# A gated SSD layer: when each group's gate is normed and scaled, where its x tiles lie, and when the sample state is loaded

## The chip, the cores and the metric

The kernel runs on one NeuronCore of a Trainium2 chip. The metric is the device time of one execution in microseconds (us). Five engines work beside each other: TensorE (PE; its weight loads are listed apart as PEld), VectorE (DVE), ScalarE (ACT), GpSimd (POOL) and SyncE (SP). In this kernel every DMA is issued by SyncE, in the order of its instruction list. Each engine runs its own list in order and waits on semaphores for the others.

## The reference

One step of a streaming encoder with two layers, over a prompt of 1024 tokens and a sample chunk of 32 tokens that share all weights. Layer 0 mixes with a Mamba-2 SSD scan, layer 1 with stick-breaking attention; each is followed by a squared-ReLU MLP. The change lies in layer 0, whose mixer is, cut short:

```python
zxbcdt = u @ in_w                                   # z 2048, x 2048, B 1024, C 1024, dt 32 columns
xbc, new_conv = causal_conv(xbc, conv_state, conv_w, conv_b)      # 4 taps, then silu
# per chunk, heads in 8 groups of 4, h is the state of a head:
y_diag = einsum('btsg,btsgr,bsgrp->btgrp', cb, decay, xdt_c)
y_off  = einsum('btgn,bgrpn,btgr->btgrp', c_c, h, exp(a_cs))
h_new  = h * exp(a_cs[:, -1]) + einsum('bsgn,bsgr,bsgrp->bgrpn', b_c, decay_end, xdt_c)
y = (y + d_skip * x_h) * silu(z)                    # the gate
yg = y.reshape(bsz, seqlen, SSD_GROUPS, 256)
yg = yg * rsqrt(mean(yg * yg, axis=-1) + EPS)       # norm over a group's 256 columns
return (yg * norm_w) @ out_w, new_conv, h_new
```

The scan starts from zero for the prompt and from the given `ssm_state` for the sample. Both final states are outputs.

## The kernel before

**Tiling.** Everything is kept transposed: a tile is 128 features by 1056 tokens (1024 of the prompt, 32 of the sample). A float32 product is done in three passes over a high and a low half of both operands (L184), so one tile of the input projection, for 128 output features, is 8 x 3 x 3 = 72 matmuls of 128x352: three token groups of 24, each into its own PSUM tile `ps_i`. `gemm` returns such a tile as six thunks of 12 matmuls, two for each token group; the evacuation follows in the second. Ahead of the first, the weights are loaded (`ws_i`) and split into halves by ScalarE (L143) and GpSimd (L144).

**Groups.** The layer has eight groups of four heads. Group g needs six projection tiles: B, C, x0 and x1 (`conv_tile`) and z0 and z1 (`z_tile`). `conv_tile` multiplies by `rstd` into a padded row `pre` (L409, L412), runs the four taps (ScalarE L423, VectorE L425 twice, L427 and L428) and silu as a tanh (L429, L430). Its result `s_<g><kind>` goes to one of eight tiles h0 to h7, four for even groups and four for odd ones. The tap sums, the tanh of z and the gate's scratch `gs` share the tag "cv", which has two buffers.

**Scan.** `scan_thunks(g)` walks nine chunks, eight of 128 prompt tokens and chunk 8 with the sample's 32. `stage_a(c)` puts C times B and the transposes of x0, x1 and B into one PSUM tile `pa` (L469 to L472) and makes from it the decay matrix L, the scaled inputs `xd`, the copy `bt`, and `ab`, the decayed C (ScalarE L487, GpSimd L488). `stage_b(c)` multiplies them into `pb` (L504, L509, and L512 with the state h), adds the new state (L520), and adds the result to the x tiles in place (L523). For chunk 8 it first loads the sample's state `h0` (L497, L498) into a tile of the state's own rotation of three.

**Gate.** `gate(g)` returns three thunks: a multiplies the x tiles by z and sums their squares (GpSimd and ScalarE); b sums over the partitions on TensorE (`ss_g`), takes the reciprocal root on VectorE (L558 and the nine operations L214 to L223, each 128x264) and spreads it over all partitions through DRAM (L244 out, L247 back); c scales both x tiles (L564) and stores them to `yn_d` (L566), from where the output projection loads them after the last group.

**Order.** Iteration g of the loop at L610 makes a main list: the z tiles of group g-1, then B, C, x0 and x1 of group g+1, with the gate's thunks a, b, c of group g-1 ahead of B, C and x0. `weave` lays the 18 thunks of `scan_thunks(g)` between the 36 of the main list, starting after the third. In the last iteration z of group 7 and the first quarter of an output projection take the place of the convolutions. So the programme's order is written out here; the framework's scheduler then orders each engine's list from it, and the pools' tags decide who waits for whose buffer.

Of the kernel before, what the change touches and what calls it, by code (L numbers as in the profile page):

```python
# [7 lines left out]
F32 = mybir.dt.float32  # L8
# [10 lines left out]
T = SEQ + DEC  # L19
# [75 lines left out]
def hybrid_step(ctx: ExitStack, tc: tile.TileContext, xt, cst, cbf, w_in, w_dt, w_out, w_up0, w_dn0, w_qkv, w_o,  # L95
# [3 lines left out]
    dma = nc.sync.dma_start  # L99
# [4 lines left out]
    hx = ctx.enter_context(tc.tile_pool(name="hx", bufs=1))  # L104
# [193 lines left out]
    def ssd_layer():  # L298
# [4 lines left out]
        with st:  # L303
# [91 lines left out]
            slots = {}  # L395
            cnt = [0]

            def conv_tile(g, kind, xs=None):

                ct = {"x0": 2 * g, "x1": 2 * g + 1, "B": 16 + g, "C": 24 + g}[kind]  # L400
                slot = {"B": 0, "C": 1, "x0": 2, "x1": 3}[kind]
                fi = 6 * g + slot
                p = pre[cnt[0] % 2]
                cnt[0] += 1

                def evac(gi, ps):
                    lo, hi = gi * GW, (gi + 1) * GW
                    if hi <= SEQ:
                        ve.tensor_tensor(p[:, 3 + lo:3 + hi], ps, rstd[:, GRP[gi]], op=ALU.mult)  # L409
                    else:  # L410
                        n = SEQ - lo
                        ve.tensor_tensor(p[:, 3 + lo:3 + SEQ], ps[:, :n], rstd[:, lo:SEQ], op=ALU.mult)  # L412
                        ve.tensor_tensor(p[:, 6 + SEQ:], ps[:, n:], rstd[:, SEQ:], op=ALU.mult)
                        post()

                def post():
                    gp.tensor_copy(p[:, 3 + SEQ:6 + SEQ], cs[:, C_SC + 3 * ct:C_SC + 3 * ct + 3])
                    gp.tensor_copy(cvo[:, ct, 0:3], p[:, SEQ:SEQ + 3])
                    gp.tensor_copy(cvo[:, ct, 3:6], p[:, T + 3:T + 6])
                    n = SEQ + 3 + DEC  # L420
                    a = qp.tile([128, T + 6], F32, name=f"cv_{g}{kind}", tag="cv", bufs=2)
                    w = [cwh[:, 4 * ct + i:4 * ct + i + 1] for i in range(4)]
                    sc.activation(a[:, :n], p[:, 0:n], AF.Identity, scale=w[0], bias=cwh[:, 128 + ct:129 + ct])  # L423
                    for i in (1, 2):
                        ve.scalar_tensor_tensor(a[:, :n], p[:, i:i + n], w[i], a[:, :n], op0=ALU.mult, op1=ALU.add)  # L425
                    o = hx.tile([128, T], F32, name=f"s_{g}{kind}", tag=f"h{4 * (g % 2) + slot}")
                    ve.scalar_tensor_tensor(o[:, :SEQ], p[:, 3:3 + SEQ], w[3], a[:, :SEQ], op0=ALU.mult, op1=ALU.add)  # L427
                    ve.scalar_tensor_tensor(o[:, SEQ:], p[:, 6 + SEQ:], w[3], a[:, SEQ + 3:n], op0=ALU.mult, op1=ALU.add)  # L428
                    sc.activation(a[:, :T], o, AF.Tanh)  # L429
                    ve.scalar_tensor_tensor(o, a[:, :T], 1.0, o, op0=ALU.add, op1=ALU.mult)  # L430
                    slots[g, kind] = o

                return gemm(w_in[fi], xs or [xg[k] for k in range(KD)], pg, evac, f"i{fi}", gmajor=pa is not None or kind == "C")
# [23 lines left out]
            def scan_thunks(g):  # L457

                out = []
                box = {}  # L460

                def stage_a(c):
# [2 lines left out]
                    B, C, x0, x1 = (slots[g, k] for k in ("B", "C", "x0", "x1"))  # L465
                    ab = qp.tile([128, 4, 128], F32, name=f"ab_{g}_{c}", tag="ab", bufs=3)
                    dma(ab[:, :, :w], acs_d[4 * g:4 * g + 4, tk].partition_broadcast(128))
                    A = pa.tile([128, 512], F32, name=f"pa_{g}_{c}", tag="pa", bufs=2)
                    te.matmul(A[0:w, 0:w], B[:, tk], C[:, tk], start=True, stop=True)  # L469
                    te.transpose(A[0:w, 128:256], x0[:, tk], ident)  # L470
# [21 lines left out]
                def stage_b(c):  # L492
# [1 line left out]
                    tk = slice(128 * c, 128 * c + w)  # L494
                    L, xd, bt, ce = box.pop(c)
                    if c == 8:
                        h = qp.tile([128, 256], F32, name=f"h0_{g}", tag="hst", bufs=3)  # L497
                        dma(h, ssm0[g])  # L498
                    elif c == 0:
                        h = None  # L500
                    else:
                        h = box["h"]
# [35 lines left out]
            def gate(g):  # L538
# [1 line left out]
                ys = [slots[g, f"x{j}"] for j in range(2)]  # L540
                box = {}

                def scratch(n):
                    return qp.tile([128, T + 6], F32, name=f"{n}_{g}", tag="cv", bufs=2)[:, :T]

                def a():
                    box["s"] = [scratch(f"gs{j}") for j in range(2)]
                    e = ve if g == 7 else gp
                    for j in range(2):
                        e.tensor_tensor(ys[j], ys[j], slots[g, f"z{j}"], op=ALU.mult)  # L550
# [56 lines left out]
            def stage(b):  # L607
                return lambda i: (sp, f"pre{i}") if i < 2 else (qp, f"z{i - 2}")

            for g in range(8):  # L610
                main, side = [], scan_thunks(g)
                gt = gate(g - 1) if g > 0 else []
                if g > 0:
                    main += z_tile(g - 1, 0) + z_tile(g - 1, 1)
                if g < 7:
                    for k in ("B", "C", "x0", "x1"):
                        main += gt[0:1] + conv_tile(g + 1, k)
                        gt = gt[1:]
                else:
                    main += gt[0:1] + z_tile(7, 0) + gt[1:2] + z_tile(7, 1, False) + gt[2:3]  # L620
                    out0 = late(lambda: down_block(w_out[0], load_o(yn_d, 0, None, stage(0), 1), X, pg, "o0",
                                                   gmajor=True), 24)
# [1123 lines left out]
```

## Time and profile before

| what | number |
| --- | --- |
| median of three runs | 3028.87 us (3023.06 to 3031.92) |
| the profiled execution | 3030.64 us |
| its span, first to last instruction | 3028.8 us |
| mean granted clock of TensorE | 0.992 |
| instructions | 54974 |
| HBM read, written | 240.80 MB, 96.52 MB |
| stretch 0 to 90 us (first norm, tiles of group 0), PE busy | 82.56 us |
| stretch 155 to 728 us (six of the eight groups), PE busy | 551.50 of 573.00 us |
| the same stretch: VectorE, ScalarE, GpSimd busy | 443.20, 219.59, 362.73 us |
| stretch 728 to 870 us (end of the loop, output projection), PE busy | 140.13 of 142.00 us |

A busy share is the time in which an engine ran any instruction. The granted clock is the share of full speed that TensorE's throttle allowed; the trace gives it for windows of some 3.4 us. TensorE is the busiest engine of the loop, so what matters there is where it waits and at which clock it runs; a wait is read as the idle time ahead of an instruction with the instruction that ended it, printed as [us <-engine tile line].

### The profile page before, as it was taken

Reading aid. Unit: us, or ns where it says so; the run is one execution under the profiler, and the core shown is the slowest. Engines: PE = TensorE matmul, PEld = TensorE weight load, DVE = VectorE, ACT = ScalarE, POOL = GpSimd, SP = SyncE. Lnnn points to the kernel's source line nnn. Section 1 sums busy time; section 2 is a strip of 40 time slices with the busy share of each in tenths; the row PEclk is TensorE's granted clock in tenths of the full one; section 3 lists DMA queues with packets and bytes.
Section 4 is the critical chain, followed back from the end, with each engine's and each line's share of the span. In section 5 each row is a group of like instructions: output and inputs, shape, how many; then the busy total and the mean of one; then the engine's idle time right before and its main releaser. Section 6 shows DMA issues by size and latency. Waiting matters only on the chain.

```text
span 3028.8 us, 54974 instructions
## 1 busy us (share of the span) xinstructions
PE 2948.6 (97%) x22262; PEld 2800.2 (92%) x22262; DVE 2287.4 (76%) x3327; ACT 1291.2 (43%) x2207; POOL 645.9 (21%) x525
## 2 busy tenths in 40 slices
PE   9999999999999999999999999999999999999999
PEld 7899888998899999999998888888889999989999
DVE  7877787777847877788776577677777977788776
ACT  4433434333323433344333466666664433344331
POOL 2766666666200000000000023323230000000000
PEclk9999999999999999999999999999999999999999
DMA  4323333233532444365432322222234444465442
GB/s 135 75 69 79 70 84 83 75 73 105 179 115 99 154 157 142 124 199 165 142 111 101 90 82 75 66 77 67 65 113 159 145 148 153 135 200 160 134 132 76
DMA packets 185589, 349.28 MB, mean 115 GB/s; under 512 B 21132, under 2 KB 78328, under 8 KB 185336
## 3 DMA queue, kind: packets, MB, share of 16 engines
q1 hardware_dynamic: 185336, 345.77, 37.2%
q8 instruction: 175, 2.87, 0.4%
q14 instruction: 78, 0.64, 0.1%
HBM read 240.80 MB, written 96.52 MB: 111 GB/s over the span
## 4 chain that ended last, share of the span: by engine, by line
PE 76%; DVE 15%; issue 3%; DMA 3%; ACT 2%; POOL 0%; SPq 0%; DVEq 0%; ACTq 0%; POOLq 0%
PE ps_i L185 10%; PE ps_ua L878 9%; PE ps_ub L878 9%; PE ps_o L185 3%; PE ps_q L185 3%; PE ps_k L185 2%; PE o L1424 2%; PE wt L1408 2%; PE ps_o L166 2%; PE ps_lb L166 2%; PE ps_la L166 2%; DVE p L1371 1%; PE ps_p L185 1%; PE ps_v L185 1%; PE pb L509 1%
## 5 line engine op out<-in xcount | busy, mean ns | idle before, releaser
L185 PE MATMUL ps_i<-xh_n,wh_i 128*128 128x352 f32 x1056 | 359.2, 340 | 0.0
L185 PE MATMUL ps_i<-xh_n,wl_i 128*128 128x352 f32 x1056 | 343.4, 325 | 0.0
L185 PE MATMUL ps_i<-xl_n,wh_i 128*128 128x352 f32 x1056 | 343.2, 325 | 0.0
L1371 DVE TENSOR_TENSOR_SCAN p<-p 128x255 f32<-128x255 f32 (+7 forms) x128 | 193.4, 1511 | 90.2 <-ACT p L1369 89.2
L1373 POOL TENSOR_TENSOR b<-b,p 128x255 f32<-128x255 f32 (+7 forms) x128 | 165.4, 1293 | 378.0 <-DVE p L1371 232.6
L185 PEld LDWEIGHTS ps_i<-xh_n,wh_i 128*128 128x128 f32 x1056 | 201.6, 191 | 13.9 <-issue 11.7
L185 PEld LDWEIGHTS ps_i<-xl_n,wh_i 128*128 128x128 f32 x1056 | 203.0, 192 | 0.0
L185 PEld LDWEIGHTS ps_i<-xh_n,wl_i 128*128 128x128 f32 x1056 | 201.1, 190 | 0.0
L1245 POOL MEMSET qs<- 128x64 f32 x8 | 1.2, 152 | 868.7 <-PE ss_a L227 852.8
L477 ACT ACTIVATE L<-L,naT 128x128 f32<-128x128 f32 (+1 forms) x288 | 89.8, 382 | 164.7 <-POOL L L474 164.7
L1369 ACT ACTIVATE p<-z,qn_q 128x384 f32<-128x384 f32 (+4 forms) x192 | 104.7, 580 | 59.4 <-PE z L1400 29.0
L144 POOL TENSOR_TENSOR wl_i<-ws_i,wh_i 128x1024 fp32r<-128x1024 f32 x44 | 106.7, 2424 | 71.3 <-ACT wh_i L143 71.1
L474 POOL TENSOR_TENSOR L<-ab,cs 128x512 f32<-128x512 f32 (+1 forms) x72 | 102.7, 1427 | 55.9 <-PE pb L509 48.1
L1408 PE MATMUL wt<-cs,b 128*128 128x128 f32 x576 | 90.3, 280 | 15.4 <-DVE wts L1413 12.8
L1369 ACT ACTIVATE b<-z,qn_q 128x384 f32<-128x384 f32 (+4 forms) x192 | 104.5, 585 | 0.0
L729 ACT ACTIVATE d_a<-y_a 128x528 fp32r<-128x528 f32 x105 | 66.8, 640 | 87.2 <-DMA y_a<-q_da 15.9
L729 ACT ACTIVATE d_b<-y_b 128x528 fp32r<-128x528 f32 x105 | 66.3, 639 | 82.1 <-DMA y_b<-q_db 11.5
L1408 PEld LDWEIGHTS wt<-cs,b 128*128 128x128 f32 x576 | 64.9, 140 | 31.2 <-DVE wts L1413 14.0
L730 DVE TENSOR_TENSOR d_a<-y_a,d_a 128x528 fp32r<-128x528 f32 x105 | 73.2, 703 | 21.3 <-ACT d_a L729 21.2
L730 DVE TENSOR_TENSOR d_b<-y_b,d_b 128x528 fp32r<-128x528 f32 x105 | 73.2, 702 | 18.4 <-ACT d_b L729 18.3
L878 PE MATMUL ps_ub<-b_b,wh_b_raw 128*128 128x264 f32 x480 | 77.2, 282 | 0.0
L878 PE MATMUL ps_ua<-b_a,wh_a_raw 128*128 128x264 f32 x480 | 77.2, 282 | 0.0
(1667 smaller groups left out, 9441.7 us busy)
## 6 DMA issues: line engine op xcount, KB each, us to landing
y_a<-q_da SPq DMA_DIRECT2D x98, 264.0 KB
y_b<-q_db SPq DMA_DIRECT2D x98, 264.0 KB
ws_i<-in_w_in SPq DMA_DIRECT2D x48, 512.0 KB
ab<-acs_d SPq DMA_DIRECT2D x64, 256.0 KB
ws_a<-in_w_up SPq DMA_DIRECT2D x30, 512.0 KB
ws_b<-in_w_up SPq DMA_DIRECT2D x30, 512.0 KB
q_da<-t_a SPq DMA_DIRECT2D x26, 528.0 KB
q_db<-t_b SPq DMA_DIRECT2D x26, 528.0 KB
```

Of the source, the lines that this page charges most:

```text
L144: eng[0].tensor_tensor(lo, st, hi.bitcast(F32), op=ALU.subtract)
L166: te.matmul(box["ps"][g][:, :GW], a[:, c:c + 128], b[:, GRP[g]], start=(k == ks[0] and i == 0), stop=(k == ks[-1] and i == 2))
L185: te.matmul(box["ps"][:, :n], a[:, c:c + 128], b[:, grp[g]], start=(k == 0 and i == 0), stop=(k == nk - 1 and i == 2))
L474: gp.tensor_tensor(L[0:w, :, :w], ab[0:w, :, :w], cs[0:w, None, C_MASK:C_MASK + w].to_broadcast([w, 4, w]), op=ALU.add)
L477: sc.activation(L[0:w, h, :w], L[0:w, h, :w], AF.Exp, bias=naT[0:w, c, 4 * g + h:4 * g + h + 1])
L729: sc.activation(hi, x, AF.Copy)
L730: ve.tensor_tensor(lo, x, hi.bitcast(F32), op=ALU.subtract)
L878: te.matmul(ps[:, g, :QW], a[:, c:c + 128], b[:, QW * g:QW * g + QW], start=(first and n == 0 and i == 0), stop=(n == len(ks) - 1 and i == 2),
L1369: sc.activation(t[0:np_, c:c + w], ps[0:np_, :w], AF.Sigmoid, scale=sn[0:np_, f])
L1371: ve.tensor_tensor_scan(p[0:np_, 1:W][:, ::-1], p[0:np_, 1:W][:, ::-1], p[0:np_, 1:W][:, ::-1], 1.0, op0=ALU.mult, op1=ALU.bypass)
L1373: gp.tensor_tensor(b[0:np_, 0:W - 1], b[0:np_, 0:W - 1], p[0:np_, 1:W], op=ALU.mult)
L1408: te.transpose(ps[:, c, :], self.b[:, 128 * (c0 + c):128 * (c0 + c) + 128], ident)
```

## The change

It touches four things, all in `ssd_layer()`. What is computed stays the same.

1. The x tiles of a group rotate over three sets of two tiles (`XT`), where they had two sets: h2 and h3, h6 and h7, and a new pair in the pool `qp`. B and C keep their two sets.
2. The sample's state has a tile of its own, and its load is issued in `stage_a(4)` instead of in `stage_b(8)`.
3. The gate's scratch `gs0` and `gs1` have tiles of their own and no longer share "cv" with the convolutions.
4. Thunk a of a group's gate stays ahead of the next B tile. Thunks b and c wait for the next iteration, where they stand behind the first two thunks (24 matmuls) of the two z tiles.

```diff
--- before.py
+++ after.py
@@ -395,6 +395,8 @@
             slots = {}
             cnt = [0]
 
+            XT = [[(hx, "h2"), (hx, "h3")], [(hx, "h6"), (hx, "h7")], [(qp, "x20"), (qp, "x21")]]
+
             def conv_tile(g, kind, xs=None):
 
                 ct = {"x0": 2 * g, "x1": 2 * g + 1, "B": 16 + g, "C": 24 + g}[kind]
@@ -423,7 +425,8 @@
                     sc.activation(a[:, :n], p[:, 0:n], AF.Identity, scale=w[0], bias=cwh[:, 128 + ct:129 + ct])
                     for i in (1, 2):
                         ve.scalar_tensor_tensor(a[:, :n], p[:, i:i + n], w[i], a[:, :n], op0=ALU.mult, op1=ALU.add)
-                    o = hx.tile([128, T], F32, name=f"s_{g}{kind}", tag=f"h{4 * (g % 2) + slot}")
+                    pool, tag = (hx, f"h{4 * (g % 2) + slot}") if slot < 2 else XT[g % 3][slot - 2]
+                    o = pool.tile([128, T], F32, name=f"s_{g}{kind}", tag=tag, bufs=1)
                     ve.scalar_tensor_tensor(o[:, :SEQ], p[:, 3:3 + SEQ], w[3], a[:, :SEQ], op0=ALU.mult, op1=ALU.add)
                     ve.scalar_tensor_tensor(o[:, SEQ:], p[:, 6 + SEQ:], w[3], a[:, SEQ + 3:n], op0=ALU.mult, op1=ALU.add)
                     sc.activation(a[:, :T], o, AF.Tanh)
@@ -465,6 +468,9 @@
                     B, C, x0, x1 = (slots[g, k] for k in ("B", "C", "x0", "x1"))
                     ab = qp.tile([128, 4, 128], F32, name=f"ab_{g}_{c}", tag="ab", bufs=3)
                     dma(ab[:, :, :w], acs_d[4 * g:4 * g + 4, tk].partition_broadcast(128))
+                    if c == 4:
+                        box["h0"] = qp.tile([128, 256], F32, name=f"h0_{g}", tag="h0", bufs=1)
+                        dma(box["h0"], ssm0[g])
                     A = pa.tile([128, 512], F32, name=f"pa_{g}_{c}", tag="pa", bufs=2)
                     te.matmul(A[0:w, 0:w], B[:, tk], C[:, tk], start=True, stop=True)
                     te.transpose(A[0:w, 128:256], x0[:, tk], ident)
@@ -494,8 +500,7 @@
                     tk = slice(128 * c, 128 * c + w)
                     L, xd, bt, ce = box.pop(c)
                     if c == 8:
-                        h = qp.tile([128, 256], F32, name=f"h0_{g}", tag="hst", bufs=3)
-                        dma(h, ssm0[g])
+                        h = box["h0"]
                     elif c == 0:
                         h = None
                     else:
@@ -540,11 +545,8 @@
                 ys = [slots[g, f"x{j}"] for j in range(2)]
                 box = {}
 
-                def scratch(n):
-                    return qp.tile([128, T + 6], F32, name=f"{n}_{g}", tag="cv", bufs=2)[:, :T]
-
                 def a():
-                    box["s"] = [scratch(f"gs{j}") for j in range(2)]
+                    box["s"] = [qp.tile([128, T], F32, name=f"gs{j}_{g}", tag=f"gs{j}", bufs=1) for j in range(2)]
                     e = ve if g == 7 else gp
                     for j in range(2):
                         e.tensor_tensor(ys[j], ys[j], slots[g, f"z{j}"], op=ALU.mult)
@@ -607,16 +609,23 @@
             def stage(b):
                 return lambda i: (sp, f"pre{i}") if i < 2 else (qp, f"z{i - 2}")
 
+            gates = []
             for g in range(8):
                 main, side = [], scan_thunks(g)
-                gt = gate(g - 1) if g > 0 else []
                 if g > 0:
-                    main += z_tile(g - 1, 0) + z_tile(g - 1, 1)
+
+                    for j in range(2):
+                        z = z_tile(g - 1, j)
+                        main += z[:2] + gates[:1] + z[2:]
+                        gates = gates[1:]
+                    gates = gate(g - 1)
                 if g < 7:
                     for k in ("B", "C", "x0", "x1"):
-                        main += gt[0:1] + conv_tile(g + 1, k)
-                        gt = gt[1:]
+                        if k == "B" and gates:
+                            main.append(gates.pop(0))
+                        main += conv_tile(g + 1, k)
                 else:
+                    gt = gates
                     main += gt[0:1] + z_tile(7, 0) + gt[1:2] + z_tile(7, 1, False) + gt[2:3]
                     out0 = late(lambda: down_block(w_out[0], load_o(yn_d, 0, None, stage(0), 1), X, pg, "o0",
                                                    gmajor=True), 24)
```

From L409 on, the changed kernel's lines have moved by two to nine: L430 is now L433, L425 is L427, L448 is L451, L469 to L472 are L475 to L478, L478 is L484, L482 is L488, L520 is L525, L558 is L560, L564 is L566. L214 to L223 kept their numbers.

**The start of a group, TensorE.** These are TensorE's instructions around the first transposes of group 5, before: `ps_i` are the z tiles of group 4, `pa_0` is chunk 0, and L471 transposes x1, the last tile that the convolutions finished.

```order
L185 MATMUL ps_i_2_5242<-xh_n_233,wh_i_5185 128x352
L185 MATMUL ps_i_2_5242<-xl_n_234,wh_i_5185 128x352
L185 MATMUL ps_i_2_5242<-xh_n_233,wl_i_5186 128x352
L469 MATMUL pa_0_5257<-s_5C,s_5B 128x128
L470 MATMUL pa_0_5257<-cs,s_5x_5008 128x128
L471 MATMUL pa_0_5257<-cs,s_5x_5159 128x128
L472 MATMUL pa_0_5257<-cs,s_5B 128x128
L185 MATMUL ps_i_2_5242<-xh_n_262,wh_i_5185 128x352
```

The same place after the change; the second fence is the row sum of group 3's gate, which now stands a little ahead of it, between two token groups of the z tile.

```order
L185 MATMUL ps_i_1_5212<-xh_n_343,wh_i_5162 128x352
L185 MATMUL ps_i_1_5212<-xl_n_344,wh_i_5162 128x352
L185 MATMUL ps_i_1_5212<-xh_n_343,wl_i_5163 128x352
L475 MATMUL pa_0_5240<-s_5C,s_5B 128x128
L476 MATMUL pa_0_5240<-cs,s_5x_4987 128x128
L477 MATMUL pa_0_5240<-cs,s_5x_5138 128x128
L478 MATMUL pa_0_5240<-cs,s_5B 128x128
L185 MATMUL ps_i_2_5257<-xh_n_142,wh_i_5162 128x352
```

```order
L227 MATMUL ss_g_5193<-gs_3_4523,ones_71 32x264 x4
L185 MATMUL ps_i_1_5212<-xh_n_142,wh_i_5162 128x352
```

Between the last products of group 4 and these transposes stood two token groups of 24 matmuls and twelve of the third; now two token groups and the four matmuls of the row sum (eight records in the trace, where a float32 product takes two passes) stand there.

**The start of a group, VectorE.** Before, the end of x1's convolution stood among evacuations of z (L448):

```order
L425 SCALAR_TENSOR_TENSOR cv_5x_5155<-pre_90,cwh,cv_5x_5155 128x1059 x2
L448 SCALAR_TENSOR_TENSOR z_5214<-ps_i_0_5189,rstd 128x352
L427 SCALAR_TENSOR_TENSOR s_5x_5159<-pre_90,cwh,cv_5x_5155 128x1024
L428 SCALAR_TENSOR_TENSOR s_5x_5159<-pre_90,cwh,cv_5x_5155 128x32
L430 SCALAR_TENSOR_TENSOR s_5x_5159<-cv_5x_5155,s_5x_5159 128x1056
L448 SCALAR_TENSOR_TENSOR z_5214<-ps_i_1_5216,rstd 128x352
L478 TENSOR_TENSOR L_0_5262<-L_0_5262,pa_0_5257 128x512
```

After the change, at the same place:

```order
L427 SCALAR_TENSOR_TENSOR cv_5x_5134<-pre_90,cwh,cv_5x_5134 128x1059 x2
L451 SCALAR_TENSOR_TENSOR z_5191<-ps_i_0_5166,rstd 128x352
L430 SCALAR_TENSOR_TENSOR s_5x_5138<-pre_90,cwh,cv_5x_5134 128x1024
L431 SCALAR_TENSOR_TENSOR s_5x_5138<-pre_90,cwh,cv_5x_5134 128x32
L560 TENSOR_SCALAR gs_3_4523<-ss_g_5193 128x264
L214 TENSOR_SCALAR gs_3_4523<-gs_3_4523 128x264
L215 TENSOR_SCALAR gs_3_4523<-gs_3_4523 128x264
L216 SCALAR_TENSOR_TENSOR gs_3_4523<-gs_3_4523 128x264
L433 SCALAR_TENSOR_TENSOR s_5x_5138<-cv_5x_5134,s_5x_5138 128x1056
L217 TENSOR_TENSOR gs_3_4523<-gs_3_4523 128x264
L451 SCALAR_TENSOR_TENSOR z_5191<-ps_i_1_5212,rstd 128x352
```

Four of the ten operations of group 3's reciprocal root stand between the taps and the last operation of x1's silu; the other six follow it.

**The middle of a group, VectorE.** These are the operations ahead of chunk 5's state in group 4, before. `s_3x` under L564 is the second scaled x tile of group 3; `s_5B` and `s_5C` are the next group's tiles.

```order
L564 SCALAR_TENSOR_TENSOR s_3x_3313<-s_3x_3313,cs,gs_3_4508 128x1056
L430 SCALAR_TENSOR_TENSOR s_5B<-cv_5B,s_5B 128x1056
L478 TENSOR_TENSOR L_6_4865<-L_6_4865,pa_6_4860 128x512
L425 SCALAR_TENSOR_TENSOR cv_5C<-pre_90,cwh,cv_5C 128x1059
L482 TENSOR_TENSOR xd_6_4872<-pa_6_4860,dtT 128x256
L425 SCALAR_TENSOR_TENSOR cv_5C<-pre_90,cwh,cv_5C 128x1059
L482 TENSOR_TENSOR xd_6_4872<-pa_6_4860,ddT 128x256
L427 SCALAR_TENSOR_TENSOR s_5C<-pre_90,cwh,cv_5C 128x1024
L428 SCALAR_TENSOR_TENSOR s_5C<-pre_90,cwh,cv_5C 128x32
L409 TENSOR_TENSOR pre_89<-ps_i_0_4885,rstd 128x352
L520 TENSOR_TENSOR h_5_4921<-ht_5_4922,pb_5_4911 128x256
```

And after:

```order
L484 TENSOR_TENSOR L_6_4844<-L_6_4844,pa_6_4839 128x512
L488 TENSOR_TENSOR xd_6_4851<-pa_6_4839,dtT 128x256
L488 TENSOR_TENSOR xd_6_4851<-pa_6_4839,ddT 128x256
L427 SCALAR_TENSOR_TENSOR cv_5C<-pre_90,cwh,cv_5C 128x1059 x2
L411 TENSOR_TENSOR pre_89<-ps_i_0_4864,rstd 128x352
L430 SCALAR_TENSOR_TENSOR s_5C<-pre_90,cwh,cv_5C 128x1024
L431 SCALAR_TENSOR_TENSOR s_5C<-pre_90,cwh,cv_5C 128x32
L525 TENSOR_TENSOR h_5_4900<-ht_5_4901,pb_5_4890 128x256
```

No scaling stands there any more; the two scalings of a group now stand beside the z tiles of the next iteration.

**SyncE.** Before, the load of `h0` stood between the store of the prompt's final state (L527) and the ab loads of the next group's chunks 2 and 3, behind which came the store of the sample's final state (L529). After, the load of the next group's `h0` (L473) stands behind that store. Behind it follow a weight load, the row sums' store (L244), another weight load, the reload (L247), the two `yn` stores (L568), and then the ab load of chunk 4.

## The prediction

> **What bounds the kernel now.** I read the page first, then TensorE's own waits over the SSD groups, then the granted clock in short windows, then the timelines of the engines that end those waits.
>
> ```profile
> PE 2948.6 (97%) x22262; PEld 2800.2 (92%) x22262; DVE 2287.4 (76%) x3327; ACT 1291.2 (43%) x2207; POOL 645.9 (21%) x525
> ```
>
> TensorE is busy for 97% of the span, so a change can only win what TensorE loses by waiting, and by what waiting does to its clock. The next view lists TensorE's waits between 90 and 760 us, which is the loop over the groups: who waited for whom, us in total, times, longest.
>
> ```profile
> PE pb L512 <- DVE h L520: 8.6, 6, 1.4
> PE pb L512 <- DMA h<-in_ssm: 8.1, 7, 1.7
> PE pa L471 <- DVE s_7x L430: 2.1, 1, 2.1
> PE pb L504 <- ACT bt L485: 1.7, 6, 0.3
> PE pa L471 <- DVE s_5x L430: 0.5, 1, 0.5
> ```
>
> The first and the fourth row come once in each of six groups, in the middle of it; the second at each group's end (the sample state); the third and fifth at the start of a group, where the transposes wait for the last x tile. The windows below (length, then busy us of PE, PEld, DVE, ACT and POOL, then TensorE's granted clock) show what a wait does beside its own length.
>
> ```profile
> 145.40:148.80 3.40, 3.40 (x14) 3.40 (x13) 3.40 (x5) 1.80 (x5) 1.49 (x2) 0.50 0.76 212
> 503.80:507.20 3.40, 1.70 (x14) 0.86 (x14) 3.27 (x7) 1.43 (x3) 2.44 (x3) 1.00 0.01 2
> 507.20:510.60 3.40, 3.40 (x19) 3.07 (x16) 3.40 (x7) 0.88 (x1) 0.28 (x1) 0.50 0.28 39
> 725.67:729.08 3.41, 1.59 (x11) 1.59 (x12) 2.81 (x5) 0.47 (x1) 0.00 (x0) 1.00 0.49 159
> 729.09:732.50 3.41, 3.41 (x25) 3.41 (x24) 1.15 (x3) 1.45 (x3) 0.04 (x1) 1.00 0.00 0
> 155.15:727.93 572.78, 551.28 (x3825) 511.87 (x3825) 443.16 (x666) 219.59 (x426) 362.73 (x274) 0.98 0.33 80
> ```
>
> After the window with the mid-group wait, in which TensorE was busy for only 1.70 us, the clock is halved for 3.4 us: 1.7 us of progress are lost. After the wait of 2.1 us at 725, which two windows share, it stays at 1.00. The last row holds six groups, 95.5 us each. Its clock of 0.98 leaves 2% of 572.8, some 11 us, for half-clock stretches, which is one of 1.7 in each group (10.2). The first row is one more, behind the first wait for the sample state.
>
> **What the present waits cost.** A wait's loss is the distance between two starts, less what the same pair takes where nothing waits.
>
> ```profile
> 504.96 0.44 PE L509 MATMUL pb<-L,xd 128*64 128x128 f32 x4
> 506.83 0.44 PE L512 MATMUL pb<-ab,h 128*64 128x128 f32 x4 [1.43 <-DVE h L520]
> ...
> 518.17 0.44 PE L509 MATMUL pb<-L,xd 128*64 128x128 f32 x4
> 518.43 0.39 PE L512 MATMUL pb<-ab,h 128*64 128x128 f32 x4
> ```
>
> Mid-group: 1.87 less 0.26 is 1.6, with 0.3 for bt 1.9, with the clock 3.6; six groups, **21.6**.
>
> ```profile
> 523.86 0.30 PE L509 MATMUL pb<-L,xd 32*64 32x32 f32 x4
> 525.24 0.31 PE L512 MATMUL pb<-ab,h 128*64 128x32 f32 x4 [1.08 <-DMA h<-in_ssm]
> ...
> 535.92 0.27 PE L470 MATMUL pa<-cs,s_5x 128*128 128x128 f32 x1
> 536.74 0.33 PE L471 MATMUL pa<-cs,s_5x 128*128 128x128 f32 x1 [0.54 <-DVE s_5x L430]
> ```
>
> Sample state: 8.1 in all, 1.7 of it in the first group (with its clock window 3.4), the other six 6.4: **9.8**. Last x tile: some 0.7 in each of five groups (0.82 less about 0.1 for a transpose that does not wait, since four matmuls of the rows above take 0.26 from start to start) and 2.2 in the last: **5.7**. Together 37.1 us, which is all that can be won here.
>
> **The change part by part.** *Sample state.* The order puts its load behind the store of the previous group's state, so it lands a group ahead; 9.8 goes. What is late next is the x1 chain below.
>
> *Gate out of the middle.* Before, two scalings stood between chunk 5's state and its predecessors; one of them is here:
>
> ```profile
> 495.27 3.22 DVE L564 SCALAR_TENSOR_TENSOR s_3x<-s_3x,cs,gs 128x1056 f32<-128x1056 f32 x1
> ```
>
> With the rsqrt ahead of it that is the backlog that made the h of row 506.83 late. Now only convolution and scan stand there, as in the x stretch at 518, where the same pair does not wait. VectorE is busy for 443 of the 573 us of six groups and has 21.6 free in each. The moved work is ten rsqrt operations, four of them quoted below (1.45 to 2.84 together), and at most 6.4 of scaling. It finds room beside the z tiles if half of the free time lies there, which no view of before can show. I take all of the 21.6 as won; at worst none of it goes (a rival).
>
> *Three x sets, own scratch.* The scratch no longer holds the convolutions' buffers, and x0 of the next group finds its buffers free. That frees ScalarE and VectorE, not a wait of TensorE: 0, inside what was already counted.
>
> *SyncE's queue.* The store and reload of the row sums and the two yn stores now stand ahead of the fifth ab load, and one weight load stands between store and reload. The ab load needs a buffer that chunk 1 frees at about that time, and weights are fetched more than a tile ahead, so 0. If that cover goes, the two scalings wait for the reload, with the scan's next L, xd and h queued behind them on VectorE; that is the second rival's price.
>
> *Start of a group: the new price.* There the rsqrt now lies in the way. The chain to the last x tile before the change (VectorE, ScalarE, GpSimd):
>
> ```profile
> 526.14 0.42 DVE L520 TENSOR_TENSOR h<-ht,pb 128x256 f32<-128x256 f32 x1 [2.21 <-PE pb L512]
> 526.48 0.40 DVE L523 SCALAR_TENSOR_TENSOR s_4x<-s_4x,cs,pb 128x32 f32<-128x32 f32 x2
> 526.79 5.08 DVE L425 SCALAR_TENSOR_TENSOR cv_5x<-pre,cwh,cv_5x 128x1059 f32<-128x1059 f32 x2
> 531.80 0.51 DVE L448 SCALAR_TENSOR_TENSOR z<-ps_i,rstd 128x352 f32<-128x352 f32 x1
> 532.24 1.87 DVE L427 SCALAR_TENSOR_TENSOR s_5x<-pre,cwh,cv_5x 128x1024 f32<-128x1024 f32 x1
> 534.03 0.24 DVE L428 SCALAR_TENSOR_TENSOR s_5x<-pre,cwh,cv_5x 128x32 f32<-128x32 f32 x1
> 535.42 1.26 DVE L430 SCALAR_TENSOR_TENSOR s_5x<-cv_5x,s_5x 128x1056 f32<-128x1056 f32 x1 [1.15 <-ACT cv_5x L429]
> ```
>
> ```profile
> 524.15 1.25 ACT L423 ACTIVATE cv_5x<-pre,cwh 128x1059 f32<-128x1059 f32 x1
> ```
>
> ```profile
> 528.37 2.40 POOL L144 TENSOR_TENSOR wl_i<-ws_i,wh_i 128x1024 fp32r<-128x1024 f32 x1
> 530.72 2.31 POOL L488 TENSOR_TENSOR ab<-ab,s_5C 128x512 f32<-128x512 f32 x1
> ```
>
> VectorE's and GpSimd's large SBUF operations take turns here: the second of the two L425 ends 1.1 us after L144 does, and L488 takes 2.31 where it starts beside it. [...]
>
> Without the wait for the state, TensorE starts L512 at 524.0 and h is out at 525.3, so L425 may start at 525.5, when the activation is done (525.4). GpSimd then has L144 next, then L488; whichever is first, the pair of L425 ends near 530.1 to 531.3 instead of 531.87, L427 at 532.4 to 532.9, and L428 at 532.7 to 533.1: the chain comes 1.1 to 1.5 earlier. Between L428 and L430 stand four new operations:
>
> ```profile
> L558 DVE TENSOR_SCALAR gs<-ss_g x8: 420/422/433, 188.4 to 810.6; 128x264 f32<-128x264 f32 x8
> L214 DVE TENSOR_SCALAR gs<-gs x8: 300/1684/1700, 188.8 to 811.1; 128x264 int32<-128x264 int32 x8
> L215 DVE TENSOR_SCALAR gs<-gs x8: 297/298/299, 190.6 to 811.4; 128x264 int32<-128x264 int32 x8
> L216 DVE SCALAR_TENSOR_TENSOR gs<-gs x8: 427/433/435, 190.9 to 811.7; 128x264 f32<-128x264 f32 x8
> ```
>
> That is 1.45 us with L214 at its least and 2.84 at its median; 1.15 of it falls into the wait for ScalarE. GpSimd should have nothing to do there, so I take the least: L430 starts at 534.3 to 534.5 and the transpose at 535.6. L558 waits for the row sums, which TensorE has summed by 529.
>
> TensorE gets there earlier than before. Only 48 in-projection matmuls and the row sums stand ahead of the transposes, instead of 60:
>
> ```profile
> 537.18 3.84 PE ps_i L185 x24
> ```
>
> ```profile
> L227 PE MATMUL ss_g<-gs,ones x64: 385/400/413, 186.9 to 810.1; 128*32 128x264 f32 x64
> ```
>
> The first row is from the chain of waits, the second from the tile's own view. 24 take 3.84, so twelve fewer are 1.9, and the eight records of a group's row sums, which overlap like their neighbours, about 0.7. TensorE would start L471 at 536.0 (its time without the wait) less 1.2 (state), less 1.9, plus 0.7: 533.6. It waits 2.0, in each of six groups: **12.0** to be paid. Bounds: nothing if the chain shrinks by 2 more, 4.8 each if nothing shrinks and L214 takes its median (536.74 plus 1.7, less 533.6).
>
> *Clock.* A 2.0 wait halves the clock if it falls within one window (row 503.80), not if two share it (row 725.67). I take one or two of six, **2.5**; bounds 0 and 10.2. [...]
>
> *Last group.* The scaling of group 6 moves behind chunk 7's operations on VectorE; behind it hang two stores and the loads of X, for which the output projection waits.
>
> ```profile
> 785.26 1.30 DVE L564 SCALAR_TENSOR_TENSOR s_6x<-s_6x,cs,gs 128x1056 f32<-128x1056 f32 x1
> ```
>
> Nothing there shows the new order. It can cost as much as two such scalings at their slower rate (3.22 each, 6.4), or win the size of one mid-group wait (1.4). I take **2.0**, between the pair at 1.30 each and nothing.
>
> **Sum.** 37.1 less 12.0, 2.5 and 2.0 is 20.6 us. The profiled execution took 3030.6 us and its span 3028.8; the median of the three runs is 3028.9, so the median should fall to about 3008.
>
> **The rivals.**
> *The clock follows the wait* (15 in 100): all six waits at the start of a group fall within windows; 10.2 instead of 2.5, so 3016. For it: one group took a whole number of windows so far, the same place being hit six times. Against it: row 725.67.
> *The backlog stays* (12): VectorE is as late in the middle as before, because the moved work with GpSimd's turns fills the z stretch and runs over. The middle keeps 21.6 and the start still pays: about 3030. So would a change that only renames the wait.
> *The start of a group becomes the bound* (7): the chain to the last x tile is no shorter, and L214 meets GpSimd each time: 4.8 and a halved window, 6.5 in six groups are 39; with 2.0 at the end 41 against 37.1, **slower**, about 3033. It decides from about 4.1 us of waiting in each group. For it: L214's median; against: in this place GpSimd's last operation before the change ended before VectorE's.
> *No new wait* (11): with turns in its favour the chain shrinks by 2 more and TensorE never waits: 35 of the 37 are kept, 2994.
>
> **How the numbers follow.** The forecast has 55 in 100, its own range 3001 to 3013. Taking in the first rival and most of the neighbours, the range is 2996 to 3026. A measurement of this kernel can tell about 0.3%, 9 us, from no change. Faster by more than that: forecast, first and last rival, less their edges, 0.77; within it 0.15; slower 0.08.
>
> **What would show it.** In the profile of the changed kernel TensorE's waits for the sample state and for h in the middle are gone, and the clock in a group's middle is 1.00. A wait of about 2 us for the last x tile stands at the start of groups 2 to 7, and VectorE runs L560, L214 to L216 right ahead of it. Wrong would be a wait for h or bt that stays, L214 at 1.7 there, a halved clock at each start, or a wait for X above 3 us at the end.

## The result and the profile after

The changed kernel takes 3010.96 us (median of six runs, 3009.16 to 3012.49) against 3028.45 for the kernel before (3023.06 to 3031.92): a ratio of 0.9935, 95% interval 0.9925 to 0.9946. The profiled executions are 3010.28 and 3030.64 us, 20.4 apart; the forecast was 20.6 between them and 3008 for the median. All of it has been gained when the MLP behind the layer starts. The view of the tile `ps_la`, its first matmuls, before and after (shortest, median and longest in ns, then first and last start in us):

```profile
L166 PE MATMUL ps_la<-yh_la,wh_la x96: 319/322/327, 928.4 to 973.3; 128*128 128x352 f32 x96
```

```profile
L166 PE MATMUL ps_la<-yh_la,wh_la x96: 319/322/327, 907.7 to 952.7; 128*128 128x352 f32 x96
```

The start of these matmuls is the measure for the traces below, since what lies behind it, which none of the edits touches, took 2096 to 2107 us in the profiled executions. TensorE's waits after, over the same stretch of 90 to 760 us as before:

```profile
PE pa L477 <- DVE s_2x L433: 2.9, 1, 2.9
PE pa L477 <- DVE s_3x L433: 1.8, 1, 1.8
PE pa L477 <- DVE s_4x L433: 1.8, 1, 1.8
PE pa L477 <- DVE s_5x L433: 1.8, 1, 1.8
PE pa L477 <- DVE s_7x L433: 1.8, 1, 1.8
PE pa L477 <- DVE s_6x L433: 1.8, 1, 1.8
PE pa L477 <- DVE s_1x L433: 1.5, 1, 1.5
```

The waits for the sample state, for h in the middle and for bt are gone. One wait is left in each group, for the last x tile at its start. VectorE's timeline at the start of group 5 shows the chain ahead of it:

```profile
514.66 1.88 DVE L430 SCALAR_TENSOR_TENSOR s_5x<-pre,cwh,cv_5x 128x1024 f32<-128x1024 f32 x1
516.46 0.24 DVE L431 SCALAR_TENSOR_TENSOR s_5x<-pre,cwh,cv_5x 128x32 f32<-128x32 f32 x1
516.62 0.42 DVE L560 TENSOR_SCALAR gs<-ss_g 128x264 f32<-128x264 f32 x1
517.08 0.30 DVE L214 TENSOR_SCALAR gs<-gs 128x264 int32<-128x264 int32 x1
517.41 0.30 DVE L215 TENSOR_SCALAR gs<-gs 128x264 int32<-128x264 int32 x1
517.75 0.43 DVE L216 SCALAR_TENSOR_TENSOR gs<-gs 128x264 f32<-128x264 f32 x1
518.10 1.25 DVE L433 SCALAR_TENSOR_TENSOR s_5x<-cv_5x,s_5x 128x1056 f32<-128x1056 f32 x1
```

The four root operations stand between L431 and L433 and take 1.48 us from start to start, each at its least duration. The new loss is at the end of the loop, in group 7's last chunk and right behind it (TensorE, then GpSimd, then VectorE beside it):

```profile
770.78 0.31 PE L517 MATMUL pb<-ab,h 128*64 128x32 f32 x4 [2.22 <-POOL ab L494]
...
773.55 0.66 PE L185 MATMUL ps_o<-xh_y,wh_o 128*128 128x352 f32 x1 [1.87 <-DVE X_in_xt L658]
```

```profile
766.25 4.47 POOL L494 TENSOR_TENSOR ab<-ab,s_7C 128x128 f32<-128x128 f32 x1 [1.50 <-ACT ab L493]
```

```profile
766.87 1.20 DVE L144 TENSOR_TENSOR wl_o<-ws_o,wh_o 128x1024 fp32r<-128x1024 f32 x1
768.00 2.41 DVE L205 TENSOR_TENSOR xl_y<-yl_sp,xh_y 128x1056 fp32r<-128x1056 f32 x2
```

One small GpSimd operation took 4.47 us and ends 0.3 us after VectorE's three large ones do. The same one in GpSimd's timeline before:

```profile
790.48 0.47 POOL L488 TENSOR_TENSOR ab<-ab,s_7C 128x128 f32<-128x128 f32 x1 [1.33 <-ACT ab L487]
```

### The profile page after: what moved, and what is told of

It reads as the page before. It is cut to its first block, busy times and chain, and to the rows that moved or that the text cites. A ratio compares the mean times of both kernels' runs of the same rounds, so it can differ in the third digit from the quotient of the medians.

```text
span 3008.4 us, 54983 instructions
## 1 busy us (share of the span) xinstructions
PE 2939.5 (98%) x22262; PEld 2795.8 (93%) x22262; DVE 2270.4 (75%) x3327; ACT 1288.4 (43%) x2207; POOL 626.3 (21%) x525
## 3 DMA queue, kind: packets, MB, share of 16 engines
q8 instruction: 175, 2.87, 0.4%
## 4 chain that ended last, share of the span: by engine, by line
PE 82%; DVE 11%; issue 2%; DMA 2%; ACT 2%; POOL 0%; SPq 0%; DVEq 0%; ACTq 0%; POOLq 0%
PE ps_i L185 15%; PE ps_ua L887 9%; PE ps_ub L887 9%; PE ps_o L185 3%; PE ps_q L185 3%; PE ps_k L185 2%; PE o L1433 2%; PE wt L1417 2%; PE ps_o L166 2%; PE ps_v L185 2%; PE ps_lb L166 2%; PE ps_la L166 2%; PE ps_p L185 1%; DVE p L1380 1%; PE pb L514 1%
## 5 line engine op out<-in xcount | busy, mean ns | idle before, releaser
L144 POOL TENSOR_TENSOR wl_i<-ws_i,wh_i 128x1024 fp32r<-128x1024 f32 x44 | 106.8, 2428 | 73.5 <-ACT wh_i L143 73.2
```

What stands on the lines that cost most here:

```text
L144: eng[0].tensor_tensor(lo, st, hi.bitcast(F32), op=ALU.subtract)
```

## The experiments

Ratios are to the kernel before, timed on the same chip in the same rounds. The chips of e1 to e4, e5 to e8 and e9 to e12 differ, so kernels are compared by their ratios. The last column is the start of `ps_la` in the profiled execution; those of e2, e5, e7, e9 and e12 also lost one half-clock window, 1.7 us, between 83 and 90 us, at the loop's start.

| kernel | ratio (95% interval) | `ps_la` starts |
| --- | --- | --- |
| before | 1 | 928.4 |
| changed | 0.9935 (0.9925 to 0.9946) | 907.7 |
| e1: before + early h0 | 0.9953 (0.9941 to 0.9965) | 909.4 |
| e9: e1 + own scratch | 0.9932 (0.9917 to 0.9946) | 911.1 |
| e2: changed, gate's order undone | 0.9934 (0.9922 to 0.9946) | 911.3 |
| e6: changed, early h0 undone | 0.9959 (0.9945 to 0.9973) | 919.3 |
| e3: changed, root later | 0.9908 (0.9894 to 0.9921) | 905.4 |
| e11: changed, scan one thunk later | 0.9916 (0.9902 to 0.9930) | 901.7 |
| e4: changed, one operation on VectorE | 0.9931 (0.9916 to 0.9945) | 909.0 |
| e7: e4 + x sets in another order | 0.9918 (0.9903 to 0.9933) | 904.5 |
| e8: e3 + e7's edits | 0.9888 (0.9872 to 0.9905) | 898.8 |
| e12: e11 + e7's edits | 0.9899 (0.9885 to 0.9912) | 898.6 |
| e5: e1 + 52 matmuls | 0.9965 (0.9953 to 0.9978) | 920.7 |
| e10: e1 + 80 matmuls | 0.9972 (0.9963 to 0.9982) | 917.9 |

### The parts alone: e1, e2, e6, e9

e1 adds this to the kernel before:

```diff
+                    if c == 4:
+                        box["h0"] = qp.tile([128, 256], F32, name=f"h0_{g}", tag="h0", bufs=1)
+                        dma(box["h0"], ssm0[g])
...
-                        h = qp.tile([128, 256], F32, name=f"h0_{g}", tag="hst", bufs=3)
-                        dma(h, ssm0[g])
+                        h = box["h0"]
```

> The kernel before with part 2 alone: h0 has its own tile and its load is issued in stage_a(4). Theory (the parts add up): the waits for the sample state (8.1 us) and the first group's halved window go, and some of the gain is taken back at the start of the groups, where TensorE then reaches the last x tile up to 1.1 us earlier; the mid-group waits for h (8.6 us, with a halved window in each group) stay. 5 to 10 us less than before, so 3018 to 3023. Rival (the group locks to a whole number of clock windows): the period stays at 95.6 us, the gain is given back in longer waits for the last x tile, and the time is that of before within 3 us.

e2 is the changed kernel with the loop's main list written as before:

```diff
-                    for j in range(2):
-                        z = z_tile(g - 1, j)
-                        main += z[:2] + gates[:1] + z[2:]
-                        gates = gates[1:]
-                    gates = gate(g - 1)
+                    main += z_tile(g - 1, 0) + z_tile(g - 1, 1)
...
-                        if k == "B" and gates:
-                            main.append(gates.pop(0))
-                        main += conv_tile(g + 1, k)
+                        main += gt[0:1] + conv_tile(g + 1, k)
+                        gt = gt[1:]
```

> The changed kernel with the gate's thunks b and c back in the same iteration, ahead of C and x0: three x sets, own scratch and the early h0 stay. Theory: it is the scaling's and the root's place that makes the mid-group wait, so TensorE waits again for h in the middle of the groups, about 8 us in all with halved windows, and the time is that of part 2 alone within 4 us (3017 to 3024). Rival: the shared scratch made VectorE late; then the mid-group waits are gone here too and the time is at or below that of the changed kernel, 3011, since no root lies ahead of the last x tile.

e6 is the changed kernel with e1's edit taken back.

> The changed kernel with part 2 undone: h0 is again loaded in stage_b(8). Theory (a wait costs its own length, less what a later wait gives up): 1.1 us of waiting comes back at the end of seven groups, the last x tile's chain moves with it, and no windows are halved in step, since a group takes about 92.9 us, 27.2 windows; 5 to 9 us more than the changed kernel, 3016 to 3020. Rival (the wait for the sample state is what costs the clock): a halved window in most groups, 15 to 20 us more, 3026 to 3031.

e9 is e1 with this edit (the definition of `scratch` goes too):

```diff
-                    box["s"] = [scratch(f"gs{j}") for j in range(2)]
+                    box["s"] = [qp.tile([128, T], F32, name=f"gs{j}_{g}", tag=f"gs{j}", bufs=1) for j in range(2)]
```

> The kernel before with part 2 and part 3 alone: h0 early, and gs0 and gs1 in tiles of their own; two x sets, the gate's thunks where they were. Theory (the shared scratch held the convolutions of B and C behind the root and the scaling): the mid-group waits for h fall from 9.2 us in all (part 2 alone) to 4 to 5, as in e2 with 3.8, and the ratio to the kernel before is that of e2, 0.992 to 0.995. Rival (it was the third x set that let VectorE get ahead): the mid-group waits stay at 9 us.

The first rows of TensorE's waits between 90 and 760 us, in e1, e9 and e6:

```profile
PE pb L514 <- DVE h L522: 8.6, 6, 1.4
PE pa L474 <- DVE s_7x L430: 2.1, 1, 2.1
PE pb L506 <- ACT bt L488: 1.7, 6, 0.3
```

```profile
PE pa L474 <- DVE s_7x L430: 4.3, 1, 4.3
PE pb L514 <- DVE h L522: 3.0, 5, 1.0
```

```profile
PE pb L515 <- DMA h<-in_ssm: 6.5, 6, 1.6
PE pa L474 <- DVE s_3x L433: 2.0, 1, 2.0
```

In **e1** the mid-group waits are what they were, 8.6 and 1.7 us, and yet 19 of the 20.6 us to `ps_la` are gained (14 us by the ratio). The waits for the sample state were 8.1. The rest is the clock: over this stretch the kernel before has seven halved windows and e1 has one, and the same mid-group wait of 1.43 us now halves the clock in one group of six. Two of these groups, each the window with the wait and the next one (columns as in the prediction's windows):

```profile
493.28:496.69 3.41, 1.98 (x21) 1.43 (x21) 3.28 (x6) 2.03 (x2) 1.70 (x2) 1.00 0.01 2
496.69:500.10 3.41, 3.41 (x22) 3.23 (x21) 3.41 (x11) 0.78 (x2) 0.63 (x2) 1.00 0.49 71
677.60:681.01 3.41, 1.71 (x13) 0.85 (x13) 3.35 (x6) 1.32 (x3) 2.45 (x3) 1.00 0.01 2
681.01:684.42 3.41, 3.41 (x20) 3.08 (x17) 3.34 (x7) 0.98 (x2) 0.38 (x1) 0.50 0.29 33
```

A group of e1 takes 92.72 us, 27.16 windows, so the wait moves on by 0.16 window with each group. Only once is TensorE left with as little as 1.71 us of busy time in a window; beside the other five waits no window has less than 1.90. Before, 95.45 us were 27.96 windows, the wait came back to nearly the same place, and a window with 1.64 to 1.74 us of busy time stood in each group. In **e6**, with the scaling gone from the middle and 6.5 us of state waits back, the changed kernel loses 11.6 us to `ps_la` (7 by the ratio). That is the theory's price; but five windows between 140 and 720 us are halved, three of them behind the wait for the last x tile, so the rival was right that the clock suffers, not about where.

In **e9** the mid-group waits fall from 8.6 to 3.0 us with the gate where it was and two x sets; **e2** has 3.8. ScalarE's first taps of group 5's B and C tiles show why, in e1 and in e9:

```profile
473.94 1.27 ACT L423 ACTIVATE cv_5B<-pre,cwh 128x1059 f32<-128x1059 f32 x1 [4.62 <-DVE pre L409]
486.99 1.27 ACT L423 ACTIVATE cv_5C<-pre,cwh 128x1059 f32<-128x1059 f32 x1 [3.41 <-DVE s_3x L566]
```

```profile
459.74 1.26 ACT L423 ACTIVATE cv_5B<-pre,cwh 128x1059 f32<-128x1059 f32 x1
478.81 1.26 ACT L423 ACTIVATE cv_5C<-pre,cwh 128x1059 f32<-128x1059 f32 x1
```

Group 4 starts at 428.8 in e1 and 426.0 in e9, so B's convolution begins 11.5 us earlier in the group with own scratch and C's 5.5. In e1 C's first tap waits for L566, the scaling that frees the shared buffer. B's row names L409, but that is an evacuation for C; what B lacked is the first scratch tile, which is stored to DRAM then (the reload that follows the store, L247, is issued at 473.87, and group 2's B has the same wait, 4.7 us, put down to the store). Both e9 and e2 give part of it back at the end of the loop (a wait of 4.3 us for s_7x, 4.9 for X, and three or four halved windows). By the ratio e9, e2 and the changed kernel are the same: the new order and the third x set, as they stand, added nothing that these runs can tell.

### The start of a group: e3, e11

e3 moves thunk b behind five thunks of z0 instead of two; e11 makes `weave` start one thunk later in groups 1 to 6.

```diff
-                        main += z[:2] + gates[:1] + z[2:]
+                        main += z[:5 - 3 * j] + gates[:1] + z[5 - 3 * j:]
```

> The changed kernel with thunk b three thunks later in the z tile, behind chunk 0's transposes: the root's operations stand behind the last operation of x1, and 60 projection matmuls stand ahead of the transposes again. Theory (the new wait comes from the missing 12 matmuls and the four root operations): the seven waits for the last x tile, 1.5 to 2.9 us each, fall to under 0.5 each, and the kernel takes 9 to 13 us less than the changed one, 2998 to 3002. Rival (the wait only moves): the row sums' round trip lands 2 to 3 us later, the two scalings hold up chunk 1's state, and TensorE waits up to 2 us in each group for that h instead; the time stays within 4 us of the changed kernel.

```diff
-                weave(main, side, 2 if g == 7 else 3)
+                weave(main, side, 2 if g == 7 else 4 if g else 3)
```

> The changed kernel with the scan laid one thunk later into the main list in groups 1 to 6: 60 projection matmuls and the row sums stand ahead of chunk 0's transposes again, and the four root operations still stand ahead of the last operation of x1. Theory (the new wait is that of the 12 missing matmuls): the waits of 1.8 us for the last x tile fall to under 0.3 in groups 2 to 6, and the ratio to the kernel before is that of e3, 0.990 to 0.992. Rival (the root operations set it): over 1.2 us of each wait stays, and the ratio is that of the changed kernel, 0.993 to 0.995.

The wait for the last x tile at the start of groups 3 and 5, in e3 and in e11:

```profile
PE pa L477 <- DVE s_3x L433: 0.5, 1, 0.5
...
PE pa L477 <- DVE s_5x L433: 0.5, 1, 0.5
```

```profile
PE pa L477 <- DVE s_3x L433: 1.0, 1, 1.0
...
PE pa L477 <- DVE s_5x L433: 1.0, 1, 1.0
```

Of the 1.83 us, 0.9 go with the 12 matmuls alone (e11); with the root operations moved too, 0.5 are left (e3), as before the change. So the missing matmuls make 0.9 of the wait and the place of the root with its row sums 0.4 to 0.5; e11's theory and its rival each hold in part. Both kernels gain, 8 us and 6 us by the ratio. No wait of 2 us in each group took its place in e3: its rival fell. But its theory, under 0.5 us for all seven, missed three of them: 1.5 us is left in groups 1 and 2 and 2.1 in group 7, where e11 has 2.9.

### The end of the loop: e4, e7, e8, e12

e4 moves the 4.47 us operation; e7 adds the second edit:

```diff
-                        gp.tensor_tensor(ab[:, :, :w], ab[:, :, :w],
+                        (ve if g == 7 and c == 8 else gp).tensor_tensor(ab[:, :, :w], ab[:, :, :w],
```

```diff
-            XT = [[(hx, "h2"), (hx, "h3")], [(hx, "h6"), (hx, "h7")], [(qp, "x20"), (qp, "x21")]]
+            XT = [[(qp, "x20"), (qp, "x21")], [(hx, "h6"), (hx, "h7")], [(hx, "h2"), (hx, "h3")]]
```

> The changed kernel with one operation moved: chunk 8 of group 7 decays C on VectorE instead of GpSimd, where it took 4.47 us in the trace of the changed kernel against 0.47 before. Theory (GpSimd was locked out by VectorE's weight split and two y splits): both waits at the end of the loop, 2.2 us for ab and 1.9 us for X, go, and with them the two halved windows; the MLP's first matmul comes 4 to 7 us earlier. Rival (the loads of X, behind the later stores of y, set the second wait): the wait of 1.9 us for X stays or grows, and the gain is 1 to 3 us.

> The changed kernel with the decay of chunk 8 in group 7 on VectorE, as in e4, and the three x sets in another order, so that group 6 has the new pair of tiles: the first two tiles of X then take the buffers of group 5 and need not wait for group 6's scaled x tiles to be stored. Theory (the loads of X behind the late scaling set the wait at the end): both waits are gone, no window is halved there, the MLP's first matmul comes 5 to 7 us earlier than in the changed kernel (901 to 903 us), and the time is 3004 to 3006. Rival (another operation on VectorE's list, the y splits ahead of X's sum, sets it): a wait of 2 us or more for X's sum stays, and the gain is under 3 us.

> The root behind chunk 0's transposes (e3) together with e7's two edits. Theory (the two ends are independent): the waits for the last x tile stay at 0.5 us as in e3 and the end of the loop has no wait over 1 us; the sum of both gains, 5 us less than e3, 2995 to 2998. Rival (with the start free, the tail's chain is late anyway): the X wait stays at 3 us and the time is that of e3, 3001.

> e11 with e7's two edits for the end of the loop. Theory (the two ends are independent): no wait over 1 us for ab or X at the end, and a ratio 0.0015 to 0.0025 below that of e11, which would be that of e8 (0.9888) or a little less. Rival (the later scan meets the end of the loop elsewhere): the ratio is that of e11.

e4's waits between 720 and 800 us; below it, e8's. In e7 there is none in that stretch.

```profile
PE ps_o L185 <- DVE X_in_xt L658: 3.1, 1, 3.1
```

```profile
PE pb L517 <- DVE h L525: 1.3, 1, 1.3
PE pb L509 <- ACT bt L491: 0.6, 1, 0.6
```

e4 took the wait for ab away, and the one for X grew from 1.9 to 3.1: its rival held, and the ratio did not move. With X's first tiles in other buffers than group 6's x tiles (e7) that wait is gone as well. In e3 and e11 nothing waits for ab, though the operation is still on GpSimd, and X's wait is 3.2 and 3.1 us. From group 7's first transposes to `ps_la` e7 takes 203.1 us, the changed kernel 208.9 and e4 209.3. `ps_la` starts only 3.2 us earlier than in the changed kernel, mostly since one window more was halved at e7's start. The 1.3 us for h in e8 is more than the 1 us that its theory allowed. e8 beats both kernels, by 1.1% (0.9888) and 0.5%; e12 is level with it.

### The clock by itself: e5, e10

Both are e1 with token groups whose first matmul is issued twice.

```diff
+                    if k == 0 and i == 0 and g in dup:
+                        te.matmul(box["ps"][:, :n], a[:, c:c + 128], b[:, grp[g]], start=True, stop=True)
```

> The kernel with part 2 alone, and 52 projection matmuls done twice, seven in most groups: 52 x 0.16 = 8.3 us of work that nothing needs. Theory (the clock is lost where a group takes a whole number of windows): a group takes 92.72 us there and 93.84 with the added work, 95.55 if it is throttled once, which is 28.0 windows of 3.413 us as in the kernel before; once one mid-group wait falls within a window, all later ones do. Halved windows come back in four to seven groups, and the time rises by 15 to 20 us, to 3031 to 3036. Rival (the halved windows went with the wait for the sample state itself): at most two come back, and the time rises by the work alone, 8 us, to 3024.

> As e5, with 80 instead of 52 projection matmuls done twice, eleven in most groups: 28 x 0.16 = 4.5 us more work than e5. A throttled group took 94.8 us in e5 and would take 95.5 here, 28.0 windows, and one that is not throttled 93.9. Theory (a group that takes a whole number of windows when throttled stays throttled): from the first hit on every group is hit; four or more halved windows among groups 2 to 6, and 8 to 14 us more than e5. Rival (hits come by chance, whatever the period): one to three halved windows, and 4 to 6 us more than e5, the work alone.

In the middle of groups 1 to 6, e5 has one halved window and e10 none, with these waits:

```profile
PE pb L518 <- DVE h L526: 8.6, 6, 1.4
```

```profile
PE pb L518 <- DVE h L526: 8.2, 6, 1.4
```

Neither brought the step back, and both rivals' counts were nearer; the time rose by less than the added work (3.6 us over e1 and 2.1 over e5 by the ratios, for 8.3 and 4.5). But neither reached the period that it was made for: unthrottled groups took 93.3 and 93.4 us, since part of the added work filled waits (those of 0.5 us for the last x tile are gone in both). So that a whole number of windows keeps a kernel throttled is not shown. What is shown is that the same wait of 1.4 us costs a halved window in six groups of six (before), one (e1), one (e5) and none (e10).

## Why the prediction was right

**Total:** 20.6 was forecast, 20.4 came between the profiled executions and 17.5 between the medians; the time lies in the forecast's own range. The mechanism was right in its outline: the old waits went, and a new one of about 2 us stood at the start of each group behind the root's operations. That the total came out so close is luck: up to group 7's last transposes the loop won 4.3 us more than the terms gave it, and its end lost 4.3 us more. The terms are another matter.

**Sample state, 9.8:** the waits went, and e1 shows that their end alone gains 14 to 19 us. The term was too small, because the clock of the middle hung on it too.

**Gate out of the middle, 21.6:** here the step "I take all of the 21.6 as won" gave the order what other parts do. The waits did go. But 10.2 of it was clock, and e1 gets nearly all of that with every mid-group wait in place; and 5.6 of the 8.6 us for h went with the scratch (e9). Undoing the order (e2) leaves the ratio where it is, so the order, put at 21.6 less the 12.0 of the next price, gained nothing that these runs can tell.

**Three x sets, own scratch, 0:** this step failed, "That frees ScalarE and VectorE, not a wait of TensorE". The row to read was the idle time of L423 for L564 in ScalarE's view: the gate's scratch held the buffers of B's and C's taps. The third set adds nothing by itself (e2 against e9). The new order without it was not tried: group g+1's x tiles would take buffers that the scaling of group g-1 still needs.

**Start of a group, 12.0:** the six waits of groups 2 to 7 are 2.9 and five times 1.8, 12.0 together. The root's 1.45 measured 1.48. The twelve missing matmuls were put at 1.9 of each wait, less 0.7 for the row sums; giving them back with the row sums in place took 0.9 off it (e11).

**Clock, 2.5:** one window at a group's start is halved, behind the longest wait; five waits of 1.8 us lay across two windows. First group 2, then group 5, each with the window behind it:

```profile
238.72:242.13 3.41, 0.73 (x6) 0.49 (x4) 3.31 (x6) 1.08 (x1) 0.98 (x2) 1.00 0.35 131
242.13:245.55 3.42, 3.23 (x12) 3.23 (x13) 3.42 (x10) 0.12 (x1) 0.00 (x0) 0.50 0.00 0
515.20:518.61 3.41, 2.37 (x16) 2.13 (x14) 3.31 (x7) 1.09 (x1) 1.38 (x2) 1.00 0.23 91
518.61:522.03 3.42, 2.63 (x17) 2.63 (x18) 3.42 (x9) 0.00 (x0) 0.00 (x0) 1.00 0.00 0
```

So the first rival, six halved windows, was perhaps nearer than it looks: an unthrottled group takes 91.87 us, 26.9 windows, so the wait moved by only 0.085 window with each group and lay across two windows five times running. The prediction's condition, a wait within one window, is not enough by itself: three of e1's waits of 1.43 us lie within one window, and no window behind them is halved (493.28 is one). Windows were halved behind waits of 1.43 (before) and 2.87 us (changed).

**Last group, 2.0:** 6.3 were lost there. From group 7's last transposes to `ps_la` the gain shrinks from 26.9 to 20.6 us. The scaling, the stores and the loads of X were the named chain and are real (e4, e7), but ahead of them stood GpSimd's 4.47 us, which the prediction did not see; two halved windows, 3.4 us, came with these waits, and e4, without that operation on GpSimd, still has them.

**The rivals:** that the backlog stays, that the start becomes the bound, and that no new wait comes were all wrong in mechanism. To group 7's last transposes the loop won 26.9 us where 22.6 were forecast (37.1 less 12.0 and 2.5), and its end lost 6.3 where 2.0 were.

## What to carry to other kernels

Ahead of moving work out of a busy stretch, look for what holds that work back there: here a buffer shared by tag showed as idle time of an engine that nobody calls the bottleneck, 4.6 and 3.4 us of ScalarE in each of six groups of e1. A clock loss that repeats at one place must not be booked to the wait at that place alone: the same wait of 1.4 us had a halved window behind it in six groups of six before, where a group took 95.45 us, and in one of six in e1, where it took 92.72. Test it with an edit elsewhere that changes the period. When a wait is exchanged for another, count the matmuls ahead of the new one: two small moves of the order (e3 or e11, with e7's edits) were worth more here than the large one, which was not tried by itself.

## What the runs showed of the hardware

- A GpSimd operation over 128x128 elements took 4.47 us beside three VectorE operations of 1.2 us each with two SBUF inputs, and 0.47 us without them (before, 790.48); it had started 0.6 us ahead of the first. The one that started first ended last, 0.3 us behind the third. VectorE's operations took their usual time: L144 1.20 us, where its median for `wl_o` is 1.22, and the two of L205 1.24 on average, where their median is 1.24. What held GpSimd, VectorE's operations as e4's theory has it or something else, is not shown by itself; on VectorE (e4) the operation took 0.27 us.
- The turns of VectorE and GpSimd that the prediction speaks of are its reading of durations. Before, L425 took 1.31 to 3.49 us between 155 and 728 us, and 3.49 where GpSimd's L144 (2.40) ran beside it (528.4); L488 over 128x512 took 2.31 us where it started beside that L425, and 1.28 at 454.29, where VectorE was idle. What lengthens them is not shown.
- TensorE's clock halved behind a window with 1.71 us of busy time (e1) and not behind one with 1.98. Idle time at a window's very start did not halve it in the kernel before (1.59 us busy, 725.67). Busy time alone does not give the border: a halved window followed one with 2.00 us in e6 (232.81), and none followed one with 1.78 us in the same run (430.76). Where the border lies exactly was not tried.
